# Where the time-step products, the modulation loads and the first merge stand in a two-layer attention and SSD kernel

## The chip, the cores and the metric

The kernel runs on one core of a Trainium2 chip. The metric is the device time of one execution in microseconds (us); less is better. The engines are PE (TensorE, matrix products), DVE (VectorE), ACT (ScalarE), POOL (GpSimd) and SP (SyncE, which here only starts DMA transfers). Each engine works through its own instructions strictly in their order, and waits on semaphores for the others.

## The reference, cut to what matters

```
h, hc = x, ctx                      # 1024 latent and 256 context rows of 1024
for i in (0, 1):
    shift, scale, gate = split(silu(c) @ w_ada[i] + b_ada[i])      # and the same of c_ctx
    u, uc = rms(h) * (1 + scale) + shift, rms(hc) * (1 + scale_c) + shift_c
    layer 0: q, k, v, g = split(u @ w_in); y = (windowed_attention(q, k, v) * silu(g)) @ w_out
    layer 1: z, xbc, dt = split(u @ w_in)
             xs, B, C = split(silu(conv5(xbc)))                    # 8 groups of heads
             dt = softplus(dt + bias); a = cumsum over a chunk of dt * A
             scans forward and backward over chunks of 128, started from the context's states
             y = (rms_per_group((y_f + y_b + D * xs) * silu(z)) * norm_w) @ w_out
    h = h + gate * y
out = rms(h) * final_norm_w
```

All of it is fp32. The kernel gets fp32 accuracy from three products per matrix product: each operand is split in a high and a low part (`wh`, `wl`, `uH`, `uL`).

## The kernel before, in words

Rows are kept transposed in three tiles, i = 0 and 1 (512 latent columns each) and i = 2 (256 context columns). Everything is issued from Python in one order, and a scheduler then gives each engine's queue its order; that order is fixed when the program is built. Three places matter here.

**The end of layer 0's projections and the start of attention.** `qkvg` (L571 on) loops over x = 0 to 7 for q and again for the gate g. Each `g_step` computes 24 matrix products of one tile (L246 to L248), a tanh and a product on ACT and DVE (L561, L562), and a store of the result from SP (L563, `sg<-qf`). Between the steps, `fill` issues pieces of layer 1's modulation `silu(c) @ w_ada` (`ada1`): loads of `w_ada` from SP (L192) and eight PE matmuls per piece (L195); eight small ones transpose the result (L202). The list `n = [3, 3, 3, 2]` says how many pieces follow each step. After the last step, `attention` loads the rope tables (`cos`, `sin`, L530 and L531) and the weights of its first side projections (`wr<-wg`, L239), which ACT casts (L229) and POOL subtracts (L231). POOL then clears `qz` (L721) and issues the loads of `qs` and `qz` (L635, L640) from its own queue. The first score products (L655) need these.

**The passage from layer 0 to layer 1.** The last output projection leaves 512 rows whose norm has to be taken: sums over partitions by four one-column matmuls (L363; each plain fp32 matmul leaves two records in the trace), a scale on ACT (L371), a power on POOL (L372), a diagonal `dg` on DVE (L374), its spread by an fp32 matmul (L376), a copy (L378), and eight steps of modulation (L307 to L309). Beside them the raw time steps are made: 24 products each for i = 2 and i = 0 with the weight `wdt` in a `pj` bank, and four ACT copies with bias each (L919, `dt_raw`). Then the first group's projection runs: context (L1081) and latent rows (L1091), with the time steps of i = 1 between (L1101). `dt_chain` (L921 on) computes softplus, its logarithm and the two scans on 640 columns, step by step beside the convolution taps of B (`bT`, L1003, L1007, tanh L1014, product L1015). It stores the running sums (`acs`, eight stores, L937) and the chunk totals (`eald`, twelve stores, L947 and L948) to DRAM and reads them back spread over partitions (`M`, `bw`, L1217; `eal`, L949). `merge` (L1226) joins the two masks of the first chunk on DVE, after `offset` on POOL (L1222).

**The groups.** For g = 0 to 7, PE projects B, two tiles of x, C and z (L1125) of the next group while it does the scans of this one. A transpose (L1054) of a convolved tile is evicted by ACT (L1057) into `xn` or `bn`.

Of the kernel before, what the change touches and what calls it, by code (L numbers as in the profile page):

```python
# [9 lines left out]
F32 = mybir.dt.float32  # L10
# [7 lines left out]
P = 128  # L18
# [42 lines left out]
POST = 0.5  # L61
LATE = 3.0
DTPACE = 1.0
SEGS = (1.5, 2.0, 2.0, 2.2, 2.2)
_STOP = None

# [45 lines left out]
class Kernel:  # L112
# [245 lines left out]
    def rstd_c(self, pool, acc, n, width, size=512, rout=None, dout=None):  # L358

        nc, t, ps = self.nc, self.t, self.psA  # L360
        pn = t(ps, [P, 512], F32, self.ptag)
        for b in range(n // P):
            nc.tensor.matmul(pn[:, b : b + 1], acc[:, b * P : (b + 1) * P], self.ones[:, 0:1], start=True, stop=True)  # L363
        return self.rstd_n(pool, pn, n, width, size, rout, dout)

    def rstd_n(self, pool, pn, n, width, size=512, rout=None, dout=None):

        nc, t, ps = self.nc, self.t, self.psA
        nb = n // P
        rc = t(pool, [P, 4], F32, "rc", 2)[:, :nb]  # L370
        nc.scalar.activation(rc, pn[:, :nb], AF.Identity, bias=self.eps, scale=1.0 / width)  # L371
        nc.gpsimd.tensor_tensor(rc, rc, self.half.broadcast_to([P, nb]), op=ALU.pow)  # L372
        dg = t(*(dout or (pool, [P, 512], F32, "sqt"))).rearrange("p (b n) -> p b n", b=4)[:, :nb]
        nc.vector.tensor_tensor(dg, self.ident.unsqueeze(1).broadcast_to([P, nb, P]), rc.unsqueeze(2).broadcast_to([P, nb, P]), op=ALU.mult)  # L374
        pr = t(ps, [P, 512], F32, self.ptag)
        nc.tensor.matmul(pr[:, :n], self.ones, dg.rearrange("p b n -> p (b n)"), start=True, stop=True)  # L376
# [194 lines left out]
    def qkvg(self, p, wk, wv, wvp):  # L571
# [37 lines left out]
        def fill(m):  # L609
            for f in ada[:m]:  # L610
                f()
            del ada[:m]

        n = [3, 3, 3, 2]
        for x in range(8):
            w = self.load_halves(a["wq"][x])
            for i in (2, 0):
                self.q_step(p, w, x, i)
                fill(n[x % 2 * 2 + (i == 0)])
        for x in range(8):  # L620
# [84 lines left out]
    def attention(self, c0, ckv):  # L705
# [24 lines left out]
        def out_steps(i):  # L730
# [119 lines left out]
        BUFS.update(wr=2, wh=2, wl=2)  # L850
# [70 lines left out]
    def dt_chain(self, keep, rows):  # L921
# [3 lines left out]
        nb = n // P  # L925
        dt = self.dts
        w1, w2, w3, ea = [t(p, [P, KT // 2, 256], F32, y).rearrange("p a b -> p (a b)")[:, :n] for y in ("xn4", "sz", "sz", "xn4")]
        tot = t(self.pc, [P, 8], F32, "tot", 2)[:, :nb]
        et = t(self.pc, [P, 8], F32, "tot", 2)[:, :nb]
        blocks = lambda x: x.rearrange("p (c n) -> p c n", n=P)  # L930
        v, act = nc.vector, nc.scalar.activation

        def decay():
            for o in (0, 384):
                for y in range(4):
                    d, s = y // 2, (o // 384) * 512 + 256 * (y % 2)
                    nc.sync.dma_start(self.acs_d[32 * d : 32 * d + 32, s : s + 256], w3[32 * y : 32 * y + 32, o : o + 256])  # L937

        def total():
            v.tensor_copy(tot[:64], blocks(w3)[:64, :, P - 1])  # L940
            v.tensor_copy(tot[64:], blocks(w3)[64:, :, 0])
            act(et, tot, AF.Exp)
            for y in range(4):
                d, h = y // 2, y % 2
                row = self.eal_d[0][32 * d : 32 * d + 32]
                for o, c in ((0, 2 * h), (3, 4 + 2 * h)):
                    nc.sync.dma_start(row[:, c : c + 2], et[32 * y : 32 * y + 32, o : o + 2])  # L947
                nc.sync.dma_start(row[:, 8 + h : 9 + h], et[32 * y : 32 * y + 32, 2:3])  # L948
# [5 lines left out]
        def turn(b):  # L954
# [14 lines left out]

        steps = [  # L970
            lambda: v.scalar_tensor_tensor(w1, in0=dt, scalar=-1.0, in1=dt, op0=ALU.mult, op1=ALU.min),
            lambda: act(w1, w1, AF.Exp),
            lambda: v.tensor_scalar_add(w2, w1, 1.0),
            lambda: v.tensor_scalar_add(w3, w2, -1.0),
            lambda: (act(ea, w2, AF.Ln), v.tensor_sub(w1, w1, w3)),
            lambda: v.reciprocal(w3, w2),
            lambda: v.tensor_mul(w1, w1, w3),
            lambda: v.tensor_add(w1, w1, ea),
            lambda: v.scalar_tensor_tensor(dt, in0=dt, scalar=0.0, in1=w1, op0=ALU.max, op1=ALU.add),
            lambda: v.tensor_scalar_max(w2, dt, 1.0e-38),  # L980
            lambda: (act(w2, w2, AF.Ln), v.tensor_scalar(out=w1, in0=dt, scalar1=self.aneg, scalar2=None, op0=ALU.mult)),
            lambda: v.tensor_tensor_scan(out=w3[:64], data0=keep[:64], data1=w1[:64], initial=0.0, op0=ALU.mult, op1=ALU.add),
            lambda: v.tensor_tensor_scan(out=w3[64:, ::-1], data0=keep[64:, ::-1], data1=w1[64:, ::-1], initial=0.0, op0=ALU.mult, op1=ALU.add),
            decay,
            total,
            lambda: v.tensor_sub(blocks(w1), tot.unsqueeze(2).broadcast_to([P, nb, P]), blocks(w3)),
            lambda: act(w1, w1, AF.Exp),
            lambda: v.tensor_sub(w2, w2, w3),
            lambda: v.tensor_mul(w1, w1, dt),
            lambda: act(ea, w3, AF.Exp),  # L990
            rows,
        ]
        return steps + [lambda b=b: turn(b) for b in (2, 0, 4, 3, 1)]

# [16 lines left out]
    def silu(self, raw, acc):  # L1011

        nc = self.nc
        return [lambda: nc.scalar.activation(raw, acc, AF.Tanh),  # L1014
                lambda: nc.vector.scalar_tensor_tensor(acc, in0=raw, scalar=1.0, in1=acc, op0=ALU.add, op1=ALU.mult)]  # L1015

    def front(self, g, st, post, first=None, dt=None):

# [122 lines left out]
    def ssd(self, c0):  # L1141
# [16 lines left out]
        def hd(d, g):  # L1158
            return slice(32 * d + 4 * g, 32 * d + 4 * g + 4)
# [11 lines left out]
            return xw  # L1171

        def decay(hn, h, g, c, d):
            nc.gpsimd.tensor_tensor(hn, h, self.eal[:, hd(d, g), c].unsqueeze(2).broadcast_to([P, R, HP]), op=ALU.mult)

        def flat(x):
            return x.rearrange("p r h -> p (r h)")
# [46 lines left out]
        def merge(M, bw):  # L1224

            nc.vector.copy_predicated(M, self.before.unsqueeze(1).broadcast_to([P, R, P]), bw)  # L1226
# [438 lines left out]
```

## Time and profile before

| what | us |
|---|---|
| median of 3 runs | 1812.75 |
| the three runs | 1812.54, 1812.75, 1817.5 |
| the profiled execution: its own time | 1817.81 |
| the profiled execution: its span | 1816.1 |

PE is the engine to look at: it is busy nearly all the span, so its idle stretches and the stretches at a lower granted clock are what a change can win. In the rows of the profile, a bracket after an instruction gives the idle time just before it on its engine and what ended it. `PEclk` is the granted clock of TensorE, 1.00 being full speed.

### The profile page before, as it was taken

The numbers are of one execution on the slowest core, as the hardware profiler recorded it, in microseconds if no ns is written. First come the engines' busy times: TensorE is split into PE (matmuls) and PEld (weight loads), VectorE is DVE, ScalarE is ACT, GpSimd is POOL, SyncE is SP. The second block draws the span as 40 slices with busy tenths as digits, with TensorE's granted clock in tenths as the row PEclk, the third lists the DMA queues.
The fourth block names the chain that finished last, engine by engine and source line by source line (L and its number), as shares of the span: only waits on it lengthen the run. The fifth ranks groups of instructions, "written<-read, shape, count | busy, mean of one in ns | idle before, by whom it ended". The sixth has DMA issues, their size and how long they took to land. (4 is left out here: it accounts for less than half of the span.)

```text
span 1816.1 us, 28983 instructions
## 1 busy us (share of the span) xinstructions
PE 1745.0 (96%) x10319; PEld 1500.2 (83%) x10319; DVE 1180.8 (65%) x2116; ACT 866.3 (48%) x1904; POOL 798.6 (44%) x1068
## 2 busy tenths in 40 slices
PE   6899999999999999999999999999999999999997
PEld 2697778888888887778898898989889898988886
DVE  4634426788877885684776757577675757767643
ACT  3612227777777774462444534344443434544522
POOL 2331117555575555103454545545454554554321
PEclk9999999999999999999999999999999999999998
DMA  9658856434454446222333323323333332656542
GB/s 327 230 144 258 275 177 154 111 96 105 115 151 129 122 108 220 73 52 72 75 74 82 92 70 86 79 76 77 81 93 73 82 79 77 185 163 179 165 135 70
DMA packets 212495, 227.61 MB, mean 125 GB/s; under 512 B 16384, under 2 KB 149632, under 8 KB 212352
## 3 DMA queue, kind: packets, MB, share of 16 engines
q1 hardware_dynamic: 178288, 207.12, 38.4%
q0 software_dynamic: 34064, 18.65, 5.7%
q8 instruction: 81, 1.33, 0.3%
q14 instruction: 62, 0.51, 0.1%
HBM read 190.88 MB, written 35.13 MB: 124 GB/s over the span
## 5 line engine op out<-in xcount | busy, mean ns | idle before, releaser
L246 PE MATMUL pj<-uH,wh 128*128 128x512 f32 (+1 forms) x712 | 259.3, 366 | 10.9 <-ACT uH L466 6.3
L247 PE MATMUL pj<-uL,wh 128*128 128x512 f32 (+1 forms) x712 | 245.1, 345 | 0.5 <-POOL uL L703 0.4
L248 PE MATMUL pj<-uH,wl 128*128 128x512 f32 (+1 forms) x712 | 244.5, 344 | 0.4 <-POOL wl L231 0.4
L1091 PE MATMUL pj<-uH,wl 128*128 128x512 f32 x512 | 172.8, 406 | 0.0
L1091 PE MATMUL pj<-uH,wh 128*128 128x512 f32 x512 | 171.5, 405 | 1.2 <-ACT bn L1057 0.7
L1091 PE MATMUL pj<-uL,wh 128*128 128x512 f32 x512 | 169.2, 403 | 0.0
L246 PEld LDWEIGHTS pj<-uH,wh 128*128 128x128 f32 x712 | 137.3, 193 | 37.8 <-ACT uH L466 7.7
L1125 PE MATMUL pj<-wh,uH 128*128 128x256 f32 x512 | 150.3, 294 | 9.1 <-ACT xn L1057 9.1
L1169 POOL TENSOR_TENSOR xw<-xn,dtdec 128x256 f32<-128x256 f32 x144 | 92.6, 648 | 141.4 <-PE psD L1194 106.8
L1125 PE MATMUL pj<-wh,uL 128*128 128x256 f32 x512 | 152.7, 298 | 0.0
L248 PEld LDWEIGHTS pj<-uH,wl 128*128 128x128 f32 x712 | 136.9, 192 | 18.4 <-issue 1.7
L247 PEld LDWEIGHTS pj<-uL,wh 128*128 128x128 f32 x712 | 137.5, 193 | 16.0 <-issue 3.0
L1125 PE MATMUL pj<-wl,uH 128*128 128x256 f32 x512 | 146.7, 286 | 0.0
L685 DVE TENSOR_TENSOR pl<-pt,ph 128x512 fp32r<-128x512 f32 x168 | 114.1, 688 | 47.3 <-ACT ph L684 46.3
L231 POOL TENSOR_TENSOR wl<-wr,wh 128x512 fp32r<-128x512 f32 x76 | 100.1, 1321 | 91.5 <-ACT wh L229 90.4
L659 DVE CUSTOM_DVE_ANT_0 sm<-S,mask,nsink 128x640 f32<-128x640 f32 (+2 forms) x160 | 119.2, 772 | 19.7 <-PE S L655 12.6
L661 ACT ACTIVATE sm<-sm,nm 128x640 f32<-128x640 f32 (+2 forms) x160 | 118.7, 742 | 16.5 <-DVE nm L659 15.8
L684 ACT CAST ph<-pt 128x512 fp32r<-128x512 f32 x168 | 97.4, 585 | 56.3 <-PE pt L680 52.9
L229 ACT CAST wh<-wr 128x512 fp32r<-128x512 f32 (+1 forms) x116 | 74.6, 648 | 92.1 <-PE pj L247 71.5
L1091 PEld LDWEIGHTS pj<-uH,wl 128*128 128x128 f32 x512 | 95.4, 188 | 19.1
L1091 PEld LDWEIGHTS pj<-uL,wh 128*128 128x128 f32 x512 | 95.5, 189 | 18.6
L1125 PEld LDWEIGHTS pj<-wh,uH 128*128 128x128 f32 x512 | 98.6, 193 | 13.5 <-ACT xn L1057 12.1
(338 smaller groups left out, 4815.9 us busy)
## 6 DMA issues: line engine op xcount, KB each, us to landing
wr<-w_x SPq DMA_DIRECT2D x32, 512.0 KB, 4.5
M<-acs SPq DMA_DIRECT2D x64, 256.0 KB, 5.0
bw<-acs SPq DMA_DIRECT2D x64, 256.0 KB, 5.4
wr<-w_sk SPq DMA_DIRECT2D x24, 512.0 KB, 3.7
wr<-wg SPq DMA_DIRECT2D x40, 256.0 KB, 4.5
qs<-q POOLq DMA_DIRECT2D x40, 256.0 KB, 3.9
wada<-w_ada SPq DMA_DIRECT2D x16, 512.0 KB, 7.2
wr<-wq SPq DMA_DIRECT2D x32, 256.0 KB, 2.8
```

What stands on the lines that cost most here:

```text
L229: nc.scalar.copy(h, raw)
L231: (eng or nc.vector).tensor_tensor(l, raw, h, op=ALU.subtract)
L246: self.nc.tensor.matmul(ps, lh, rh, start=first and i == 0, stop=False)
L247: self.nc.tensor.matmul(ps, lh, rl, start=False, stop=False)
L248: self.nc.tensor.matmul(ps, ll, rh, start=False, stop=last and i == n - 1)
L659: nc.vector.tensor_tensor_reduce(out=sm[:, :W], in0=Sv, in1=self.mask[:, m0 : m0 + W], scale=-SCALE, scalar=self.nsink[:, 4 * j + r : 4 * ...
L661: nc.scalar.activation(sm[:, :W], sm[:, :W], AF.Exp, bias=nm[:, r : r + 1], scale=-1.0, accum_out=sums[:, r : r + 1])
L684: nc.scalar.copy(ph, ptf)
L685: nc.vector.tensor_sub(pl, ptf, ph)
L1091: nc.tensor.matmul(raw[:, 512 * i : 512 * i + 512], l[:, k, :], r[i][:, k, :], start=k + y == 0, stop=k == KT - 1 and y == 2)
L1125: nc.tensor.matmul(pj[:, c], l, r[:, k, :], start=c % 2 + q + k + y == 0, stop=c % 2 == 1 and q == 1 and k == 3 and y == 2)
L1169: nc.gpsimd.tensor_tensor(xw, X(st, c).rearrange("p (r h) -> p r h", r=R), self.dtdec[:, c, hd(d, g)].unsqueeze(2).broadcast_to([P, R, HP] ...
```

## The change

The change has five parts.

1. The pieces of `fill` after the g steps: one behind each step for x below 4, three from x = 4 on (`late`), in place of 3, 3, 3, 2 in turn.
2. The raw time steps' products go into the score banks `S`. Those of i = 0 come in two halves, tied behind the norm's sums (`summed`) and behind its spread (`spread`), inside the list of the norm's steps.
3. The sigmoid in `dt_chain` comes from a tanh on ACT (`wr`) and two fused DVE steps, in place of a reciprocal and two products.
4. Four stores of the running sums in place of eight and two of the chunk totals in place of twelve; the totals lie in another order (`EPOS`). The rows' loads are issued ahead of the totals.
5. The first merge on DVE comes after the product that ends the convolution of C (`silu_last`).

```diff
+EPOS = (0, 1, 5, 6, 3, 4, 8, 9, 2, 7)
...
-            nc.tensor.matmul(pn[:, b : b + 1], acc[:, b * P : (b + 1) * P], self.ones[:, 0:1], start=True, stop=True)
+            self.summed = nc.tensor.matmul(pn[:, b : b + 1], acc[:, b * P : (b + 1) * P], self.ones[:, 0:1], start=True, stop=True)
...
-        nc.tensor.matmul(pr[:, :n], self.ones, dg.rearrange("p b n -> p (b n)"), start=True, stop=True)
+        self.spread = nc.tensor.matmul(pr[:, :n], self.ones, dg.rearrange("p b n -> p (b n)"), start=True, stop=True)
...
         n = [3, 3, 3, 2]
+        late = lambda x: 3 if x >= G0 else 1
...
                 self.g_step(p, w, x, i)
-                fill(n[x % 2 * 2 + (i == 0)])
+                fill(late(x))
...
-                for f in steps:
+                for f in steps[:1] + ([self.dt_first] if i == 1 else []) + steps[1:]:
...
-            for i, lo in ((2, 256), (0, 0)):
-                n = TT[i][1] // 2
-                self.dt_raw(self.dts[:, lo : lo + n], self.proj(ps, self.wdt, i), n)
+            raw = self.proj(ps, self.wdt, 2, "S")
+
+            def dt_first():
+                self.dt_raw(self.dts[:, 256:384], raw, 128)
+                out = []
+                half = self.proj_g(out, ps, [self.wdt], self.uH, self.uL, 0, "S", parts=2)
+                with self.tc.issue_after(self.summed.ins):
+                    next(half)
+                with self.tc.issue_after(self.spread.ins):
+                    next(half, None)
+                self.dt_raw(self.dts[:, :256], out[0], 256)
...
-            for o in (0, 384):
-                for y in range(4):
-                    d, s = y // 2, (o // 384) * 512 + 256 * (y % 2)
-                    nc.sync.dma_start(self.acs_d[32 * d : 32 * d + 32, s : s + 256], w3[32 * y : 32 * y + 32, o : o + 256])
+            for d in range(2):
+                for o in range(2):
+                    dst = self.acs_d[32 * d : 32 * d + 32, 512 * o : 512 * o + 512].rearrange("r (h n) -> h r n", h=2)
+                    nc.sync.dma_start(dst, w3[64 * d : 64 * d + 64, 384 * o : 384 * o + 256])
...
+            lambda: act(wr, w1, AF.Tanh, scale=-0.5),
             lambda: act(w1, w1, AF.Exp),
...
-            lambda: v.reciprocal(w3, w2),
-            lambda: v.tensor_mul(w1, w1, w3),
-            lambda: v.tensor_add(w1, w1, ea),
+            lambda: v.scalar_tensor_tensor(w1, in0=wr, scalar=1.0, in1=w1, op0=ALU.add, op1=ALU.mult),
+            lambda: v.scalar_tensor_tensor(w1, in0=w1, scalar=0.5, in1=ea, op0=ALU.mult, op1=ALU.add),
...
             decay,
+            rows,
             total,
...
-            rows,
...
-            merge(fw[0], bw.pop(0))
+        with self.tc.issue_after(self.silu_last.ins):
+            merge(fw[0], bw.pop(0))
```

What this does to the queues is shown at three places. Line numbers of the changed kernel are one to some twelve higher.

SP's queue at the start of attention, before the change. `sg_0_55<-qf_2244` is the gate of x = 4, i = 0; `sg_2_57<-qf_2295` that of x = 5, i = 2; `sg_0_55<-qf_2343` that of x = 5, i = 0. The four `wr<-wg` are the first weights of attention.

```order
L563 DMA sg_0_55_151<-qf_2244 128x512
L563 DMA sg_2_57_153<-qf_2295 128x256
L530 DMA cos_2514<-cos 128x512
L531 DMA sin_2515<-sin 128x512
L239 DMA wr_2560<-wg 128x512
L239 DMA wr_2566<-wg 128x512
L239 DMA wr_2572<-wg 128x512
L239 DMA wr_2578<-wg 128x512
L563 DMA sg_0_55_151<-qf_2343 128x512
```

The same place of SP's queue with the change; `sg_2_60<-qf_2361` is the gate of x = 6, i = 2, `sg_0_58<-qf_2396` that of x = 6, i = 0, and `sg_2_60<-qf_2454` that of x = 7, i = 2.

```order
L193 DMA wl_2400<-w_ada 128x512
L564 DMA sg_0_55_151<-qf_2310 128x512
L564 DMA sg_2_60_156<-qf_2361 128x256
L531 DMA cos_2514<-cos 128x512
L532 DMA sin_2515<-sin 128x512
L564 DMA sg_0_58_154<-qf_2396 128x512
L240 DMA wr_2560<-wg 128x512
L240 DMA wr_2566<-wg 128x512
L564 DMA sg_2_60_156<-qf_2454 128x256
L240 DMA wr_2572<-wg 128x512
L240 DMA wr_2578<-wg 128x512
```

The first two weights now stand behind the gate store of x = 6, i = 0, three projections later than before, and the next two behind that of x = 7, i = 2. The order of POOL's queue there (three subtractions, the two clears, the loads of `qs` and `qz`) is the same in both.

PE's queue around the norm's sums, before the change: the sums go straight into the 24 products of i = 0 in bank `pj_8627` (the first and last are shown), then the spread, then the first group.

```order
L248 MATMUL pj_8598<-uH_1654_6747,wdtl_8589 128x256
L363 MATMUL pt_8656<-ones_68,sqa_8275 128x1 x4
L246 MATMUL pj_8627<-uH_2034_8170,wdth_8587 128x512
...
L248 MATMUL pj_8627<-uH_2034_8170,wdtl_8589 128x512
L376 MATMUL pt_8666<-dg_2129_8664,ones_68 128x512
L1081 MATMUL psD_8771<-uH_1654_6747,wh_8765 128x256
```

With the change, twelve of the 24 stand ahead of the spread and twelve behind it, in bank `S_8643`.

```order
L249 MATMUL S_8598<-uH_1654_6747,wdtl_8589 128x256
L364 MATMUL pt_8623<-ones_68,sqa_8275 128x1 x4
L247 MATMUL S_8643<-uH_2034_8170,wdth_8587 128x512
...
L249 MATMUL S_8643<-uH_2034_8170,wdtl_8589 128x512
L377 MATMUL pt_8633<-dg_2128_8631,ones_68 128x512
L247 MATMUL S_8643<-uH_2034_8170,wdth_8587 128x512
```

DVE's queue up to the product that ends the convolution of B (`bT`), before the change: the time-step chain has come as far as the reciprocal.

```order
L1007 SCALAR_TENSOR_TENSOR bT_8798<-pj_2170_8797,cw_8721,bT_8798 128x1023
L975 TENSOR_TENSOR xn_2176_8869<-xn_2176_8869,sz_8871 128x640
L1007 SCALAR_TENSOR_TENSOR bT_8798<-pj_2170_8797,cw_8721,bT_8798 128x1022
L976 RECIPROCAL sz_8871<-sz_8870 128x640
L1015 SCALAR_TENSOR_TENSOR bT_8798<-pj_2170_8797,bT_8798 128x1024
```

With the change, the chain has gone through both scans (L991, L992) ahead of that product, and four taps of the next context tile (`cctx`) stand there too.

```order
L988 SCALAR_TENSOR_TENSOR cacc_8597<-cacc_8597,xn_2176_8869 128x640
L1016 SCALAR_TENSOR_TENSOR bT_8798<-pj_2170_8797,cw_8721,bT_8798 128x1023
L1016 SCALAR_TENSOR_TENSOR cctx_8946<-psD_8912,cw_8721,cctx_8946 128x255
L989 TENSOR_SCALAR sz_8870<-cacc_8597 128x640
L990 TENSOR_SCALAR xn_2176_8869<-cacc_8597,al_8593 128x640
L1016 SCALAR_TENSOR_TENSOR bT_8798<-pj_2170_8797,cw_8721,bT_8798 128x1022
L1016 SCALAR_TENSOR_TENSOR cctx_8946<-psD_8912,cw_8721,cctx_8946 128x255
L991 SCALAR_TENSOR_TENSOR sz_8871<-cT_8753,xn_2176_8869 64x640
L992 SCALAR_TENSOR_TENSOR sz_8871<-cT_8753,xn_2176_8869 64x640
L1016 SCALAR_TENSOR_TENSOR cctx_8946<-psD_8912,cw_8721,cctx_8946 128x254
L1025 SCALAR_TENSOR_TENSOR bT_8798<-pj_2170_8797,bT_8798 128x1024
```

More of the change, by code (lines that the diff above doesn't have):

```diff
@@ L844, in attention @@
             self.dt_setup()
-            for i, lo in ((2, 256), (0, 0)):
-                n = TT[i][1] // 2
-                self.dt_raw(self.dts[:, lo : lo + n], self.proj(ps, self.wdt, i), n)
+            raw = self.proj(ps, self.wdt, 2, "S")
[8 more added lines that the diff above has]
+                self.dt_raw(self.dts[:, :256], out[0], 256)
+            self.dt_first = dt_first
             for _ in steps[-1]():
@@ L927, in dt_chain @@
         w1, w2, w3, ea = [t(p, [P, KT // 2, 256], F32, y).rearrange("p a b -> p (a b)")[:, :n] for y in ("xn4", "sz", "sz", "xn4")]
+        wr = t(p, [P, LAT], F32, "bT")[:, :n]
         tot = t(self.pc, [P, 8], F32, "tot", 2)[:, :nb]
@@ L942, in total @@
             act(et, tot, AF.Exp)
[L943 to L948, printed above, removed]
+            for d in range(2):
+                nc.sync.dma_start(self.eal_d[0, 32 * d : 32 * d + 32].rearrange("r (h k) -> h r k", h=2), et[64 * d : 64 * d + 64])
             nc.sync.dma_start(self.eal, self.eal_d.broadcast_to([P, 64, NCH + NCC]))
@@ L1013, in silu, with prod @@
         nc = self.nc
-        return [lambda: nc.scalar.activation(raw, acc, AF.Tanh),
-                lambda: nc.vector.scalar_tensor_tensor(acc, in0=raw, scalar=1.0, in1=acc, op0=ALU.add, op1=ALU.mult)]
+        def prod():
+            self.silu_last = nc.vector.scalar_tensor_tensor(acc, in0=raw, scalar=1.0, in1=acc, op0=ALU.add, op1=ALU.mult)
+        return [lambda: nc.scalar.activation(raw, acc, AF.Tanh), prod]
     def front(self, g, st, post, first=None, dt=None):
@@ L1173, in decay @@
         def decay(hn, h, g, c, d):
-            nc.gpsimd.tensor_tensor(hn, h, self.eal[:, hd(d, g), c].unsqueeze(2).broadcast_to([P, R, HP]), op=ALU.mult)
+            nc.gpsimd.tensor_tensor(hn, h, self.eal[:, hd(d, g), EPOS[c]].unsqueeze(2).broadcast_to([P, R, HP]), op=ALU.mult)
         def flat(x):
```

## The prediction

> **What bounds the kernel now.** The first view is the page: its span and its row of PE, and the costliest group that waits regularly.
>
> ```profile
> span 1816.1 us, 28983 instructions
> PE 1745.0 (96%) x10319; PEld 1500.2 (83%) x10319; DVE 1180.8 (65%) x2116; ACT 866.3 (48%) x1904; POOL 798.6 (44%) x1068
> ...
> L1125 PE MATMUL pj<-wh,uH 128*128 128x256 f32 x512 | 150.3, 294 | 9.1 <-ACT xn L1057 9.1
> ```
>
> PE is idle for 1816.1 - 1745.0 = 71.1 us. The change adds and removes no product on PE, so only these idle times, and stretches of lower clock inside the busy time, can move the end. The second view, the waits of PE in the whole program, sorts the idle times by what ended them. These rows touch the change:
>
> ```profile
> PE pj L1125 <- ACT xn L1057: 9.1, 7, 1.3
> ...
> PE aps L195 <- DMA wl<-w_ada: 2.8, 1, 2.8
> PE pj L1054 <- DVE cacc L1015: 2.8, 2, 2.2
> ...
> PE pj L246 <- ACT cacc L919: 1.4, 1, 1.4
> PE psD L1081 <- ACT cacc L919: 1.1, 1, 1.1
> PE pj L1054 <- ACT bn L1057: 1.1, 1, 1.1
> ```
>
> One wait of 2.8 us is for a modulation load. The passage has 2.8 + 1.4 + 1.1 + 1.1, all told some 6.4 us. The groups have seven waits of 1.3 us, one in each of groups 0 to 6.
>
> **Part 1: the modulation loads.** PE's timeline at the end of layer 0's projections, and two windows of it (in a window the second last three numbers are the granted clock, the DMA share and the GB/s):
>
> ```profile
> 229.17 1.94 PE L195 MATMUL aps<-wl,cs 128*32 128x512 f32 x8 [2.84 <-DMA wl<-w_ada]
> 241.06 0.39 PE L246 MATMUL pj<-uH,wh 128*128 128x256 f32 x1
> 244.13 1.06 PE L195 MATMUL aps<-wl,cs 128*32 128x512 f32 x8
> 250.26 0.96 PE L202 MATMUL pt<-sel,qf 128*128 128x16 f32 x8
> 262.83 0.40 PE L246 MATMUL pj<-uH,wh 128*128 128x512 f32 x1
> 268.30 0.40 PE L655 MATMUL S<-kHH,qs 128*128 128x256 f32 x2
> 231.00:234.00 3.00, 3.00 (x18) 2.96 (x15) 0.00 (x0) 0.00 (x0) 0.00 (x0) 0.50 1.05 404
> 234.00:237.00 3.00, 3.00 (x12) 2.44 (x12) 0.42 (x1) 0.38 (x1) 0.00 (x0) 0.83 0.99 372
> ```
>
> PE stands 2.84 us, and from 229.17 on it runs at half clock; the second window's 0.83 puts the end of that at 234 + 1.0 = 235.0. So 5.8 us ran at half speed, which cost 2.9. With the loads spread out, each piece's load has far more time ahead of its products, and I take both losses away: PE is through with its projections at 268.30 - 2.84 - 2.9 = 262.6.
>
> But what PE does next, the first scores (L655), needs `qs`. This is its chain before, from SP's first weight load to POOL's issue, with the ACT and DVE steps of a gate:
>
> ```profile
> 246.49 7.35 SPq L239 DMA_DIRECT2D wr<-wg  x4
> ...
> 250.24 1.18 ACT L229 CAST wh<-wr 128x512 fp32r<-128x512 f32 x2 [1.60 <-DMA wr<-wg]
> 250.94 2.55 POOL L231 TENSOR_TENSOR wl<-wr,wh 128x512 fp32r<-128x512 f32 x2 [37.90 <-ACT wh L229]
> ...
> 252.16 0.59 ACT L561 ACTIVATE qf<-pj 128x512 f32<-128x512 f32 x1
> ...
> 253.96 0.68 DVE L562 SCALAR_TENSOR_TENSOR qf<-qf,pj 128x512 f32<-128x512 f32 x1
> ...
> 257.76 0.84 POOL L635 DMA_DIRECT2D qs<-q  x1
> ...
> DMA to landing us min/median/max: 3.5/5.5/5.8
> ```
>
> From the first weight's issue to the issue of `qs` pass 257.76 - 246.49 = 11.3 us: two loads, casts, POOL's subtractions, a third weight that waits for the first one's buffer, the two clears. Landing takes 5.5 to 5.8, so `qs` was there at about 263.4, 4.9 us before PE came. That slack is what the change spends. SP's queue (shown with the change) now has the first weight behind the gate store of x = 6, i = 0. Backwards from PE's end at 262.6: the last projection of 512 columns takes 268.30 - 262.83 = 5.5, that of 256 columns 244.13 - 241.06, about 3.0; the last piece's eight matmuls 1.0 and the transposes 0.8. So x = 6, i = 0 ends on PE at 262.6 - 10.3 = 252.3. Its tanh (0.59), product (0.68), the handoffs and the store's issue put the first weight at about 254.2 by my estimate, 7.7 later than before. The other link, the third weight behind the gate store of x = 7, i = 2, fits inside that: that projection ends at 256.3, its store goes out near 257.5, and the buffer comes free only near 260. So `qs` is issued near 265.5 and lands near 271.2. **PE stands about 8.6 us, and the scores start at 271.2, which is 2.9 later than 268.30.** An idle of 2.84 brought 2.9 us of half-clock loss; an idle three times as long brings at least that. Part 1 costs 2.9 + 2.9 = **+5.8 us**. Bounds: with the shortest landing seen (3.5) and no loss of clock, 0.7; with handoffs 1.3 longer, +7.1; and if the chain weren't behind the store at all, `qs` at 263.4 would leave 263.4 - 268.30 = -4.9 (the fast rival).
>
> **Part 2: the time-step products at the norm.** PE, ACT, POOL and DVE at the start of the passage:
>
> ```profile
> 741.40 0.95 PE L363 MATMUL pt<-ones,sqa 128*128 128x1 f32 x8
> ...
> 742.19 1.47 ACT L919 ACTIVATE cacc<-pj,db 32x128 f32<-32x128 f32 x4
> ...
> 744.03 1.02 POOL L372 TENSOR_TENSOR rc<-rc,half 128x4 f32<-128x4 f32 x1 [7.62 <-ACT rc L371]
> ...
> 746.05 0.69 DVE L374 TENSOR_TENSOR dg<-ident,rc 128x512 f32<-128x512 f32 x1
> ...
> 750.91 1.02 PE L376 MATMUL pt<-dg,ones 128*128 128x512 f32 x2
> 745.00:747.00 2.00, 2.00 (x6) 1.52 (x6) 1.74 (x2) 0.00 (x0) 0.04 (x1) 0.50 0.60 234
> ```
>
> In a score bank the products needn't wait for L919 to empty the `pj` bank, so the 1.4 and the 1.1 us go. Twelve products of 0.23 then run from 742.4 to 745.1, and the spread needs `dg`. The copies L919, ACT's scale, the power and the diagonal give `dg` at about 747.0: a new wait of 1.9 us, inside a stretch that loses its clock before as well (0.50). Net -0.6, PE's next row at about 752.4 rather than 753.06; -2.3 if the clock holds (then 750.8).
>
> **Part 3: the shorter softplus.** DVE in the time-step chain:
>
> ```profile
> 773.20 0.82 DVE L971 SCALAR_TENSOR_TENSOR xn<-cacc 128x640 f32<-128x640 f32 x1 [0.58 <-ACT cacc L919]
> ...
> 781.82 4.14 DVE L976 RECIPROCAL sz<-sz 128x640 f32<-128x640 f32 x1
> 785.88 1.16 DVE L1015 SCALAR_TENSOR_TENSOR bT<-pj,bT 128x1024 f32<-128x1024 f32 x1
> 786.96 0.47 DVE L1007 SCALAR_TENSOR_TENSOR cctx<-psD,cw,cctx 128x254 f32<-128x254 f32 x1
> 787.35 0.81 DVE L977 TENSOR_TENSOR xn<-xn,sz 128x640 f32<-128x640 f32 x1
> ...
> 797.81 1.47 DVE L982 TENSOR_TENSOR_SCAN sz<-cT,xn 64x640 f32<-64x640 f32 x1
> ```
>
> The reciprocal's 4.14 us leave DVE, and a tanh comes to ACT, which is busy for 48% of the span. But PE doesn't wait for the chain here: it waits for the product that ends `bT`, which is done at 785.88 + 1.16 = 787.0, and 13.8 us after the chain's first step. In the new order that stretch holds no reciprocal, but three products (0.81 each), four context taps (0.47), two narrow steps (about as long as these taps) and both scans (1.47, the second taken as the first): -4.14 + 2.4 + 1.9 + 0.9 + 3.0 = +4.1, hence 17.9. The chain starts some 2 to 3 us earlier (its input is the third set of products, which the earlier front and their place right behind `pj` move up), so `bT` is ready at about 788.5, 1.4 later than before. PE is there about 2 us earlier and stands some 4. Bounds of the delay: -1 (the taps fall into ACT's waits) and +2.
>
> **Parts 4 and 5: stores and the first merge.** SP, POOL and DVE before:
>
> ```profile
> 799.31 4.14 SPq L937 DMA_DIRECT2D acs<-sz  x8
> ...
> 819.02 1.04 POOL L1222 TENSOR_TENSOR bw<-bw,vd 128x512 f32<-128x512 f32 x1 [73.97 <-DMA bw<-acs]
> ...
> 820.09 0.73 DVE L1226 COPY_PREDICATED M<-before,bw 128x512 f32<-128x512 int32 x1 [5.11 <-POOL bw L1222]
> ...
> 822.00:825.00 3.00, 2.17 (x6) 1.21 (x6) 1.76 (x3) 3.00 (x6) 1.69 (x3) 0.52 0.46 148
> ```
>
> The merge held DVE for 5.11 us; the product of a convolved tile stood behind it, and PE's transposes waited 2.2 us for that (the row `DVE cacc L1015`), after which the clock was halved (0.52) for what I read as some 6 us, a loss of 3. The later merge takes the 2.2 and the 3 away. The stores only feed this wait, so they add nothing more. What is late next is ACT's eviction of the earlier tile, behind a cast of 1 us and a first tap: I estimate a wait of 2 us there.
>
> The passage sums to: delay at `bT` +1.4, a half clock behind that wait of 4 us +2.5, merge -5.2, eviction +2, and half of the front's -0.6 kept, -0.3. That is **+0.4**, with the bounds -6 (`bT` in time, no new loss of clock) and +3.
>
> The Trainium skill's page "TensorE: Matmul & The Clock Gate", section "HAM oscillation", says to avoid PE idle gaps above about 3.4 us, the length of the window after which the clock drops. The trace is stricter: it halved after 2.84 us and after the 2.2 of the merge, and not after the 1.3s of the groups. By the page's length the 8.6 us of part 1 cost clock and a wait somewhat shorter than my 4 at `bT` doesn't; that is the last rival.
>
> **The groups.** Nothing in the diff is aimed at them, but the scheduler's order inside a group is another: the context products of the next B come first. By its rows one eviction comes earlier than the products that wait for it, so I take the 1.3 as 1.0: 7 x -0.3 = **-2**. Bounds: all 9.1 us gone, or a second such wait in half the groups, +4.6.
>
> **The sum**: +5.8 + 0.4 - 2 = +4.2 on the profiled execution, 1817.81 + 4.2 = 1822.0. That execution is 5.1 us above the median of the three runs, so against the median the sum gives 1812.75 + 4.2 = **1817.0 us**. About 0.3% (5.4 us) is what a measurement of this kernel can tell from no change.
>
> **The rivals.**
>
> *The attention start doesn't bind.* SP's place says the weight follows the store, but if the chain behind it is shorter than I add up (POOL idle for 37.90 us before it speaks for spare time), PE goes on at 263.4 and part 1 is -4.9. With the passage at its better bound's half (-3) and the groups at -2: -9.9, 1803. Against it: the 11.3 us of chain are in the trace, and nothing in it changes.
>
> *A second wait in the groups (the slow side).* In the new order ACT takes a first tap of 1024 columns ahead of the second eviction of C's or x's tile. If PE arrives at the next products before that eviction, it waits once more per group for about as long as now, 1.3 us, 7 x 1.3 = 9.1, from the point where the eviction ends over 0 us after PE's arrival. With the 1.3s as they are: +5.8 + 0.4 + 9.1 = 15.3, 1828; with a wait of half that size, 1823.5. For it: ACT is what these waits are for already. Against it: ACT is idle half of the time.
>
> *The merge isn't what PE waits for.* If the wait for `cacc` stays (the transposes wait for the stores' effect in another way), 5.2 us don't come: 1822.
>
> *The clock holds behind the wait at `bT`.* If that wait is nearer 3 us and the clock stays (it stayed after 1.3), the 2.5 us of half clock don't come: 1814.5.
>
> **How the numbers follow.** Forecast 0.38 (1817.0, of which 0.20 within 0.3% of the median, 0.18 above it); attention start not binding 0.25 (faster); second wait in the groups 0.21 (slower); merge unchanged 0.08 (slower); clock held 0.08 (same). So faster 0.25, same 0.28, slower 0.47. The range goes from 1803, the fast rival, to 1825, a little above the slow one's smaller price; what lies beyond is about 2 in 10.
>
> **What would show each step.** Part 1: a row of L657 (the scores) with an idle of 8 to 9 us before it and `qs` or its weights as releaser, and a window at 0.50 behind it; no idle at L195. Part 2: no waits for L931's copies, one at L377 of about 2 us. Part 3: a wait of some 4 us at the first transposes (L1066). Parts 4 and 5: no idle before the merge (L1238) that PE waits for. The groups: the row of L1137 at about 7 us. It is wrong if the scores start before 266, or if PE waits in the groups for something that has no row before.

## The result, and the profile after

| kernel | median, us | runs | lowest to highest |
|---|---|---|---|
| before | 1814.79 | 4 | 1812.54 to 1817.5 |
| changed | 1834.97 | 4 | 1829.26 to 1838.53 |

The change makes the kernel slower: ratio 1.0107, with a 95% interval of 1.0085 to 1.0128. The prediction said slower as the likeliest side, but 1817.0 us and at most 1825.0. The profiled execution of the changed kernel is the fastest of its four (1829.26 us), and that of before (1817.81 us) took a little longer than any of before's four, so the two traces show 11.5 us of the 20.

The page of the changed kernel:

```profile
span 1827.6 us, 28945 instructions
PE 1748.6 (96%) x10319; PEld 1499.6 (82%) x10319; DVE 1174.1 (64%) x2115; ACT 867.1 (47%) x1903; POOL 806.3 (44%) x1068
```

PE is idle for 79.0 us (71.1 before), and the same 10319 products keep it busy 3.6 us longer. Of the waits of PE in the whole program, these are new or have changed most (the releaser, then us in all, how often, the longest):

```profile
PE S L657 <- issue: 7.5, 1, 7.5
PE psX L1264 <- POOL xw L1181: 5.7, 6, 1.0
...
PE pj L1066 <- DVE bT L1025: 3.2, 1, 3.2
PE pj L1103 <- ACT xn L1069: 3.2, 8, 1.6
PE pt L377 <- DVE dg L375: 2.6, 2, 2.1
...
PE pj L1137 <- ACT xn L1069: 2.3, 7, 0.3
```

The waits for the modulation loads at L196 and for the time-step copies are gone. In their place stand a wait before the first scores (L657), one at the spread (L377, 0.4 us before), one at `bT`'s transposes (L1066, 0.5 us before), and a new one in the groups, for POOL's `xw` (x times a decay, an operand of L1264). The groups' old wait (L1137) fell from 1.3 to 0.3 us each.

**The start of attention.** SP, POOL and PE of the changed kernel:

```profile
251.40 0.33 SPq L564 DMA_DIRECT2D sg<-qf  x1
251.82 2.12 SPq L240 DMA_DIRECT2D wr<-wg  x2
...
260.91 1.27 POOL L232 TENSOR_TENSOR wl<-wr,wh 128x512 fp32r<-128x512 f32 x1 [2.03 <-ACT wh L230]
...
263.29 0.84 POOL L637 DMA_DIRECT2D qs<-q  x1
...
267.90 0.77 PE L657 MATMUL S<-kHH,qs 128*128 128x256 f32 x2 [7.45 <-issue]
```

The first attention weight follows the gate store, `qs` is issued 263.29 - 251.82 = 11.5 us later (11.3 before), and PE stands 7.45 us. Windows of the same place:

```profile
263.00:266.00 3.00, 0.00 (x0) 0.00 (x0) 0.00 (x0) 0.00 (x0) 3.00 (x5) 0.57 0.70 208
266.00:269.00 3.00, 1.02 (x3) 0.79 (x4) 0.00 (x0) 0.00 (x0) 0.12 (x1) 0.50 1.75 225
269.00:272.00 3.00, 3.00 (x9) 2.42 (x10) 0.90 (x4) 1.09 (x4) 0.00 (x0) 0.50 0.08 5
272.00:275.00 3.00, 3.00 (x14) 2.56 (x13) 0.92 (x4) 1.53 (x5) 1.59 (x3) 0.73 0.05 9
```

By the 0.57 and the 0.73 the clock is halved from 263.4, in the middle of the idle stretch, to 273.6, nearly 6 us into the work: 10.2 us.

**The groups.** One group before, and one with the change:

```profile
1034.90:1140.70 105.80, 104.46 (x651) 93.69 (x651) 72.78 (x124) 45.09 (x106) 53.02 (x75) 1.00 0.29 81
```

```profile
1150.30:1257.40 107.10, 105.35 (x651) 93.82 (x651) 73.13 (x124) 45.43 (x106) 54.06 (x75) 1.00 0.30 79
```

The same 651 products take 1.3 us longer at full clock. PE's idle times inside this group, and the one of a group before:

```profile
1216.78 1.10 PE L1289 MATMUL psX<-xn,M 128*128 128x64 f32 x8 [0.20 <-DVE y L1268]
1239.47 0.73 PE L1103 MATMUL pj<-uH,wh 128*128 128x512 f32 x2 [0.20 <-ACT xn L1069]
1254.26 0.70 PE L1264 MATMUL psX<-xw,bn 128*128 128x256 f32 x2 [0.96 <-POOL xw L1181]
1257.35 0.39 PE L1137 MATMUL pj<-wh,uH 128*128 128x256 f32 x1 [0.34 <-ACT xn L1069]
```

```profile
1246.45 0.38 PE L1125 MATMUL pj<-wh,uH 128*128 128x256 f32 x1 [1.30 <-ACT xn L1057]
```

The idle time grows only from 1.30 to 0.20 + 0.20 + 0.96 + 0.34 = 1.70 us: the wait for `xw` is new, but the old wait lost as much. The rest of the 1.3 us is time in which the rows call PE busy; by the starts of PE's products, it lies just before these waits and once more before L1289, where a product follows the one before it later than usual. POOL and DVE where PE waits for `xw`:

```profile
1252.62 1.59 POOL L1181 TENSOR_TENSOR xw<-xn,dtdec 128x256 f32<-128x256 f32 x1
1252.32 1.42 DVE L1046 TENSOR_TENSOR wl<-wr,wh 128x1024 fp32r<-128x1024 f32 x1
```

POOL's `xw` takes 1.59 us there; the median of all 144 is some 0.61. Beside it DVE subtracts a weight's low part, with both operands in SBUF. In the trace of the changed kernel 14 of the 144 `xw` take more than 1.1 us beside such a subtraction, two in most groups, and PE waits for one of the two; in the trace of before only one does in the whole program. The order of the queues inside the groups has put the two together.

**By stage.** The marks are the starts of PE's first scores, of the norm's last sums (L363, L364) and of the z products (L1125, L1137) of groups 1 and 7, from the timelines; a column is the difference of two marks, in us. The kernels beside before and changed are those of the next section.

| kernel | to the scores | to the sums | to group 1's z | a group, mean of 6 | rest | span |
|---|---|---|---|---|---|---|
| before | 268.3 | 473.1 | 187.8 | 105.8 | 252.4 | 1816.1 |
| changed | 267.9 | 478.6 | 189.8 | 107.0 | 249.2 | 1827.6 |
| pacing alone | 275.8 | 478.2 | 187.1 | 105.8 | 252.8 | 1828.6 |
| pacing, low parts on DVE | 264.1 | 478.1 | 188.3 | 105.8 | 252.6 | 1817.7 |
| banks alone | 263.7 | 475.9 | 191.8 | 107.0 | 247.1 | 1820.5 |
| change without pacing | 264.0 | 474.8 | 190.9 | 107.0 | 247.8 | 1819.5 |
| change without banks | 273.0 | 478.6 | 189.6 | 107.1 | 249.1 | 1832.5 |
| merge alone | 266.7 | 475.0 | 182.0 | 105.8 | 250.9 | 1809.2 |

A group's period is the steadiest number: 105.8 or 107.0, nothing between. The first column isn't steady: it runs from 263.7 to 268.3 in before, the banks alone and the merge alone, whose edits all lie behind it. So part sizes are taken from the timed ratios, and the traces only for the mechanism. The first two columns together tell the pacing apart even so: 738.8 to 741.7 in the four kernels without it, 746.5 to 754.0 in the three with it, and 742.2 where the low parts are on DVE.

### The profile page after: what moved, and what is told of

Its sections match the earlier page's. It is cut to its first block, busy times and chain, and to the rows that moved or that the text cites. A ratio compares the mean times of both kernels' runs of the same rounds, so it can differ in the third digit from the quotient of the medians.

```text
span 1827.6 us, 28945 instructions
## 1 busy us (share of the span) xinstructions
PE 1748.6 (96%) x10319; PEld 1499.6 (82%) x10319; DVE 1174.1 (64%) x2115; ACT 867.1 (47%) x1903; POOL 806.3 (44%) x1068
## 5 line engine op out<-in xcount | busy, mean ns | idle before, releaser
L1181 POOL TENSOR_TENSOR xw<-xn,dtdec 128x256 f32<-128x256 f32 x144 | 106.0, 739 | 188.7 <-PE psD L1206 123.4
L1103 PE MATMUL pj<-uH,wh 128*128 128x512 f32 x512 | 166.7, 400 | 3.9 <-ACT xn L1069 3.2
L1103 PE MATMUL pj<-uH,wl 128*128 128x512 f32 x512 | 167.1, 400 | 0.0
L247 PEld LDWEIGHTS pj<-uH,wh 128*128 128x128 f32 x712 | 136.6, 192 | 37.1 <-ACT wh L230 8.0
L1137 PE MATMUL pj<-wh,uH 128*128 128x256 f32 x512 | 150.9, 295 | 2.3 <-ACT xn L1069 2.3
L1137 PE MATMUL pj<-wh,uL 128*128 128x256 f32 x512 | 148.9, 291 | 0.0
L1137 PE MATMUL pj<-wl,uH 128*128 128x256 f32 x512 | 147.1, 287 | 0.0
L1103 PEld LDWEIGHTS pj<-uH,wh 128*128 128x128 f32 x512 | 94.5, 189 | 24.0 <-ACT xn L1069 4.7
```

The lines of the kernel that those rows point to most:

```text
L247: self.nc.tensor.matmul(ps, lh, rh, start=first and i == 0, stop=False)
L1103: nc.tensor.matmul(raw[:, 512 * i : 512 * i + 512], l[:, k, :], r[i][:, k, :], start=k + y == 0, stop=k == KT - 1 and y == 2)
L1137: nc.tensor.matmul(pj[:, c], l, r[:, k, :], start=c % 2 + q + k + y == 0, stop=c % 2 == 1 and q == 1 and k == 3 and y == 2)
L1181: nc.gpsimd.tensor_tensor(xw, X(st, c).rearrange("p (r h) -> p r h", r=R), self.dtdec[:, c, hd(d, g)].unsqueeze(2).broadcast_to([P, R, HP] ...
```

## Experiments

Theory: the pacing costs by the chain from the first attention weight to `qs`; the groups cost by their queue order, whatever brings it about; the merge gains. Rivals: the scores wait for something else; the groups lose by the new layout of stores and totals, or by the banks; the softplus and the stores bring what is gained.

**Pacing alone.**

```diff
+        late = lambda x: 3 if x >= G0 else 1
-                fill(n[x % 2 * 2 + (i == 0)])
+                fill(late(x))
```

> The kernel before with the paced modulation loads alone. Theory (the chain from the first attention weight to qs binds): no idle at the modulation products, PE idle 7 to 9 us before the first scores, the clock at 0.50 for 7 to 10 us around them, the groups' period unchanged at 105.8 us; 3 to 8 us slower than before. Rival (the scores' wait comes from another part of the change): no idle there, 3 to 5 us faster.

Measured: 1828.22 us against 1815.81, ratio 1.0062 (1.0038 to 1.0086), some 11 us slower, where I had expected 3 to 8. The wait is there, and so is the clock (its waits of PE, and a window):

```profile
PE S L656 <- issue: 8.3, 1, 8.3
276.00:282.00 6.00, 5.84 (x19) 4.76 (x20) 1.82 (x8) 2.03 (x8) 0.99 (x2) 0.55 0.20 13
```

The period stays at 105.8. The theory holds, its size was too small.

**Pacing, with the low parts of the first four attention weights on DVE.** POOL's queue then has the clears and the loads of `qs` first.

```diff
-            w = self.load_halves(a[src][x], nc.gpsimd)
+            w = self.load_halves(a[src][x], nc.vector if src == "wg" and x < 2 else nc.gpsimd)
```

> The paced loads alone, and the low parts of the first four attention weights computed on DVE in place of POOL, so that POOL's queue has the two clears and the loads of qs and qz first. Theory (the first scores wait for qs, whose issue stands on POOL behind the subtractions and so behind the weights' loads): no idle above 1 us before the first scores, no half clock there; 8 to 13 us faster than the pacing alone, and -4 to +2 us against before. Rival (the wait is for something else, such as the memory of the projections' stage or the gate stores): 5 us or more of idle stay, the time within 4 us of the pacing alone.

Measured: 1816.64 us against 1816.35, ratio 1.0003 (0.9991 to 1.0015). POOL and PE of this kernel:

```profile
255.03 1.09 POOL L722 MEMSET qz<- 64x512 f32 x2 [40.61 <-issue]
256.08 0.84 POOL L636 DMA_DIRECT2D qs<-q  x1
...
264.10 0.40 PE L656 MATMUL S<-kHH,qs 128*128 128x256 f32 x2
```

`qs` is issued at 256.08, and the scores start with no idle before them. The 11 us are gone, so the chain was the whole cost of the pacing. The pacing itself then gains nothing that can be measured: before's wait for `w_ada` is 2.84 us in its one profiled execution, but 0.3 to 2.5 in the other seven kernels without pacing (the probe at the end apart), and in two of these alone the clock drops behind it.

**The same with six stores and the later merge.** The diff adds parts 4 and 5 of the change to the kernel above.

> The same with the six stores and the later first merge, without the tanh and the score banks; its groups have before's order. Theory (pacing free once qs is out of the way, merge worth about 4 us): 2 to 8 us faster than before, period 105.8. Rival (the merge's gain needs the tanh): within 2 us of the kernel with the pacing and DVE alone.

Measured: 1811.93 us against 1816.35, ratio 0.9978 (0.9966 to 0.9989). The gain comes without the tanh; whether it is the merge's or the stores' is shown further down.

**Banks alone.** Part 2 of the change, nothing else.

> The kernel before with the time-step products in the score banks alone (in two halves around the norm's spread). Theory (the queue order inside the groups, which this part alone turns into that of the changed kernel, costs the groups): period of a group 107.0 us in place of 105.8, a wait of about 1.0 us per group of the state products for POOL's xw, 7 to 10 us slower in all. Rival (the groups lose by the stores' layout or by the tanh, neither of which is in here): period 105.8, total within 3 us of before.

Measured: 1823.79 us against 1815.81, ratio 1.0033 (1.0018 to 1.0049), some 6 us slower and a little less than expected. Its waits of PE:

```profile
PE pj L1064 <- DVE bT L1025: 7.9, 1, 7.9
PE psX L1262 <- POOL xw L1179: 6.7, 7, 1.0
```

The period is 107.0 without a new layout and without a tanh, so the rival falls. The wait at `bT` is 7.9 us here, with the reciprocal still in the chain; in the whole change, with the tanh, it is 3.2. The banks have moved the time-step chain forward in DVE's queue, so that both scans stand ahead of `bT`'s product:

```profile
786.35 1.47 DVE L992 TENSOR_TENSOR_SCAN sz<-cT,xn 64x640 f32<-64x640 f32 x1
787.85 1.49 DVE L993 TENSOR_TENSOR_SCAN sz<-cT,xn 64x640 f32<-64x640 f32 x1
789.37 1.23 DVE L1025 SCALAR_TENSOR_TENSOR bT<-pj,bT 128x1024 f32<-128x1024 f32 x1
```

It is done 51.0 us after the start of the norm's sums, 45.6 before; and PE is there 2.1 us earlier.

**The change without the banks.** Parts 1, 3, 4 and 5. Its PE queue inside groups 3 to 6 is that of the changed kernel.

> The whole change without the score banks: its queues inside groups 3 to 6 are nonetheless in the changed kernel's order. Theory (the order costs, whatever part brings it about): period of a group 107.0 us, the wait for POOL's xw of 1.0 us per group is there; 14 to 20 us slower than before. Rival (the score banks themselves cost, by the memory they take or hold): period 105.8, 6 to 12 us slower.

Measured: 1834.14 us against 1816.35, ratio 1.0098 (1.0083 to 1.0113). Its waits of PE, and one group:

```profile
PE S L657 <- issue: 7.5, 1, 7.5
PE psX L1254 <- POOL xw L1171: 6.5, 7, 1.0
1155.40:1262.40 107.00, 105.28 (x650) 93.78 (x650) 73.04 (x124) 45.36 (x106) 53.95 (x75) 1.00 0.30 79
```

The period is 107.0 and the wait for `xw` is there with no bank in it. It is the order that costs, and different parts of the change lead to it. The pacing alone keeps before's order and softplus, stores and merge together keep it too; the two sets together do not. The traces leave no exception: inside groups 2 to 6 the 14 kernels have just two orders, each the same on PE, DVE, ACT and POOL. The nine with before's order have a period of 105.8 us and one or two long `xw` in the whole program; the five with the other have 107.0 us and 14 of them. The banks add nothing to this kernel that can be told from noise (1.0107 with them).

**The change without the pacing.** Parts 2 to 5.

> The whole change without the pacing. Theory (pacing costs by the chain to qs, the groups by their order, independently): no idle before the first scores, the groups' period 107.0, 5 to 12 us slower than before, and 5 to 9 us faster than the whole change. Rival (the pacing also brings the groups' order about): period 105.8, within 3 us of before.

Measured: 1821.44 us against 1815.81, ratio 1.0035 (1.002 to 1.0049). The period is 107.0 and no idle stands before the scores: pacing and order cost independently. Against the whole change that is some 13 us by the ratios, more than the 5 to 9 expected, mostly because the pacing costs more. And parts 3 to 5, which gain 4.7 us by themselves (below), gain nothing on top of the banks: 1.0035 with them, 1.0033 without.

**Softplus, stores and merge.** Parts 3, 4 and 5.

> The kernel before with the tanh in the softplus, the six stores and the later first merge, without the pacing and without the score banks; its queues inside groups 2 to 6 are in before's order on PE. Theory (order): period 105.8 us, the waits for the merge gone, 2 to 6 us faster than before. Rival (stores and totals in another layout slow POOL in the groups): period 107 us, 4 to 8 us slower.

Measured: 1810.76 us against 1815.81, ratio 0.9974 (0.9959 to 0.9988), some 4.7 us faster, period 105.8.

**Merge alone.**

```diff
-        merge(fw[0], bw.pop(0))
+        with self.tc.issue_after(self.silu_last.ins):
+            merge(fw[0], bw.pop(0))
```

> The kernel before with the later first merge alone. Theory (the merge holds DVE and so the transposes): the 2.2 us wait for cacc and often the half clock behind it go, 2 to 5 us faster than before. Rival (the shorter softplus and the stores bring the gain of parts 3 to 5): within 1 us of before.

Measured: 1808.02 us against 1816.35, ratio 0.9955 (0.9939 to 0.9972), 8 us faster and more than expected. The wait of PE for that product in this kernel, and its window at the end of the passage:

```profile
PE pj L1057 <- DVE cacc L1016: 0.6, 1, 0.6
815.00:822.00 7.00, 5.88 (x30) 4.13 (x28) 3.91 (x3) 4.27 (x7) 4.04 (x5) 1.00 0.72 136
```

The same wait was 2.8 us before, and this is before's window behind it:

```profile
822.10:828.90 6.80, 6.05 (x22) 4.55 (x23) 5.49 (x7) 3.72 (x7) 3.81 (x6) 0.50 0.64 214
```

PE was busy for 6.05 of these 6.80 us at half clock, which lost 3.0. With the 2.2 us less of waiting that is 5.2 of the 8; in this execution the clock stayed whole at the start of the passage too, where before lost 1.7.

**Merge and tanh.** Parts 3 and 5.

> The later merge and the tanh for the reciprocal, without the stores, banks and pacing; groups in before's order. Theory (the shorter softplus moves steps of the chain ahead of the taps that PE waits for, and so takes some of the merge's gain): 1 to 4 us slower than the merge alone, that is 4 to 7 us faster than before. Rival (it is the stores that take it): within 1.5 us of the merge alone.

Measured: 1811.87 us against 1814.36, ratio 0.999 (0.9976 to 1.0003); it can't be told from before, and is 3.9 us above the merge alone by the medians, and some 6 by the ratios. Waits of PE in the passage, and a window behind the second:

```profile
PE pj L1095 <- ACT bn L1061: 1.9, 1, 1.9
PE pj L1058 <- ACT bn L1061: 1.7, 1, 1.7
793.40:796.80 3.40, 3.40 (x8) 2.72 (x9) 3.34 (x4) 1.91 (x3) 0.00 (x0) 0.50 0.23 80
```

In the merge alone the same two waits are these:

```profile
PE pj L1057 <- ACT bn L1060: 1.1, 1, 1.1
...
PE pj L1094 <- ACT bn L1060: 0.7, 1, 0.7
```

With the shorter chain PE no longer waits for `bT`, but ACT, which evicts the transposes, now has a step of the time-step chain (L982) and the load of its function table ahead of the second one:

```profile
790.79 1.28 ACT L982 ACT_TABLE_LOAD   x1
792.09 0.74 ACT L982 ACTIVATE sz<-sz 128x640 f32<-128x640 f32 x1
792.73 0.57 ACT L1061 COPY bn<-pj 128x512 f32<-128x512 f32 x1
```

That is 1.8 us more of waiting, and a half clock of 3.4 us behind it. Both stand in each of the three traces with the tanh and without the banks, and in none of the three with the merge and without the tanh and the banks. So in the traces the tanh gives back part of what the merge gains, and not by the delay of `bT` that I had expected of it. The timed runs are less sure: softplus, stores and merge together have 0.9974, and the next run, which is the same without the tanh, 0.997.

**Merge and stores.** Parts 4 and 5.

> The later merge and the six stores with the rows' loads ahead of the totals, without tanh, banks and pacing; groups in before's order. Theory (with the merge out of the way nothing waits for the stores): within 1.5 us of the merge alone, 6.5 to 9.5 us faster than before. Rival (the earlier loads of the rows hold something up): 2 to 4 us slower than the merge alone.

Measured: 1808.25 us against 1814.36, ratio 0.997 (0.9956 to 0.9983); 0.2 us above the merge alone by the medians, and 2.7 by the ratios, whose intervals overlap. A cost or gain of the six stores can't be told from noise.

**Merge, and the products in the banks in one piece.**

```diff
-                self.dt_raw(self.dts[:, lo : lo + n], self.proj(ps, self.wdt, i), n)
+                self.dt_raw(self.dts[:, lo : lo + n], self.proj(ps, self.wdt, i, "S"), n)
```

> The later merge, and the time-step products in the score banks in before's place, not split around the norm's spread; its groups have the changed kernel's order on PE. Theory (the banks save the two waits of 1.4 and 1.1 us at the start of the passage, the order costs 1.2 us per group): period 107.0, the waits for the copies of the time steps gone, 2 us faster to 3 us slower than before, 6 to 11 us slower than the merge alone. Rival (only the split of the products brings the costly order about): period 105.8, 8 to 11 us faster than before.

Measured: 1825.28 us against 1814.36, ratio 1.0071 (1.0047 to 1.0095), worse than expected of either. Waits of PE:

```profile
PE psX L1255 <- POOL xw L1172: 6.7, 7, 1.0
PE pj L1057 <- DVE bT L1016: 6.2, 1, 6.2
...
PE pt L376 <- DVE dg L374: 3.8, 2, 3.4
```

The banks bring the costly order even unsplit. And both waits that they take away (1.4 and 1.1) come back larger, at the spread (3.4) and at `bT` (6.2).

**The collision by itself.** Ahead of the kernel before stands a stretch with 24 products of `xw`'s form on POOL, and beside them products and subtractions on DVE; the kernel's own work is unchanged.

```diff
+        for n in range(24):
+            nc.gpsimd.tensor_tensor(pa[n], x, f.unsqueeze(2).broadcast_to([P, 4, 64]), op=ALU.mult)
+        for n in range(8):
+            nc.vector.tensor_tensor(pm[n], acc, raw[:, :512], op=ALU.mult)      # acc in PSUM
+        for n in range(4):
+            nc.vector.tensor_sub(pl[n], raw, hi)                                # all in SBUF
```

> The kernel before with a stretch put ahead of it: 24 products on POOL of the form of xw (128x256, SBUF), and beside them on DVE first 8 products of a PSUM bank with SBUF (128x512), then 4 subtractions of the form of the weights' low part (128x1024, both operands and the result in SBUF). The total time isn't of interest. Theory (POOL's xw is slowed by a DVE subtraction that reads only SBUF, and not by one that reads PSUM): POOL's products take 0.61 us beside the PSUM products and with DVE idle, and 1.2 us or more on average beside the four subtractions. Rival (the long xw in the groups come from something else that happens at the same point, such as PE's or ACT's accesses): 0.61 us throughout.

Measured once (1825.79 us; the time isn't of interest), in groups of POOL beside the PSUM products, of POOL beside the subtractions, and of DVE:

```profile
L181 POOL TENSOR_TENSOR pa<-px,pf 128x256 f32<-128x256 f32 x9 | 5.2, 609 | 1.8 <-DVE pf L178 1.8
```

```profile
L181 POOL TENSOR_TENSOR pa<-px,pf 128x256 f32<-128x256 f32 x4 | 6.2, 1588 | 0.0
```

```profile
L188 DVE TENSOR_TENSOR pl<-praw,phi 128x1024 fp32r<-128x1024 f32 x4 | 6.1, 1591 | 0.0
L186 DVE TENSOR_TENSOR pm<-pacc,praw 128x512 f32<-128x512 f32 x8 | 4.9, 688 | 0.0
```

609 ns beside products that read PSUM, 1588 beside subtractions that read only SBUF; the 1.59 us of the group's `xw` is the same number. DVE's subtraction slows down as well, from 1.23, its median in the changed kernel, to 1.59 us. The page "SBUF — State Buffer" of the Trainium skill, section "Who interferes with whom", says that a DVE instruction with two SBUF inputs contends with a GpSimd instruction that reads SBUF. The trace agrees: in the probe the two kinds alternate, one of each every 1.55 us. They don't simply take turns, though: 0.61 and 1.23 one after the other would be 1.84. So the probe shows that the subtraction alone makes `xw` long. That removing this collision alone from the groups restores 105.8 wasn't tried; how much of the 1.3 us is the collision's, and how much the other waits of the new order, stays open.

## Why the prediction was wrong

Two steps failed: the saving that part 1 counted on, and the term of the groups.

**Part 1** was right in mechanism and too small. The chain from weight to `qs` came out at 11.5 us (11.3 forecast), the idle stretch at 7.45 (8.6), because `qs` was there 4.6 us after its issue and not 5.5 to 5.8. Of the half clock's 10.2 us, 273.6 - 267.9 = 5.7 fell into work, a loss of 2.9. That this is the 2.9 of the forecast is partly luck: it was taken over from a stretch of 6.8 us. Forecast +5.8, measured some +11 by the ratio of the pacing alone. The mis-sized term is the saving. It was taken from the one profiled execution, 2.84 us of wait and 2.9 of clock. In the seven other kernels without pacing, the probe apart, the wait is 0.3 to 2.5 us, with a mean of 1.5, and the clock stays whole there in five of them. With 1.5 of wait and no clock to save, the same sum gives 5.8 + 5.7 - 1.5 = +10.0. The fast rival, in which the attention start doesn't bind, fell with the 7.45 us of idle.

**Part 2.** The new wait at the spread is 2.1 us as forecast (1.9), and the two old waits went. The clock held there, and PE came to `bT`'s transposes 2.1 us earlier, as forecast (about 2).

**Part 3.** The wait at `bT`'s transposes is 3.2 us where I had some 4: the product is done 46.3 us after the start of the norm's sums and not 45.6, so 0.7 later (1.4 forecast). The clock was halved for 6.8 us behind it, from 792.5 on, so the rival in which it holds fell:

```profile
792.00:795.00 3.00, 1.50 (x6) 1.11 (x7) 2.94 (x6) 1.90 (x5) 0.00 (x0) 0.58 0.21 60
```

That lost 2.6 (2.5 forecast). But I put the delay down to the shorter softplus; the banks make it (a wait of 7.9 with them alone, 0.5 before), and the tanh shortens it. The tanh with the merge and no banks takes the wait at `bT` away and costs at ACT's evictions instead.

**Parts 4 and 5.** The merge's gain of 5.2 us was right in its two terms, and the merge alone measured 8. The eviction behind it waits 1.6 us (2 forecast). The stores were put at nothing, and nothing was measured that is clear of noise.

**The passage** as a whole: forecast +0.4, measured +2.0 to group 1's z in the two traces. Of that, +0.4 is up to group 0's z (832.3 - 746.5 against 826.8 - 741.4); the other 1.6 lies inside group 0.

**The groups** are the step that failed in mechanism: "By its rows one eviction comes earlier than the products that wait for it, so I take the 1.3 as 1.0: 7 x -0.3 = **-2**". That old wait did fall, to 0.3. But I looked only at the waits that existed, and the sign that I had named myself came: PE waits in the groups for something that has no row before. The new order costs 1.25 us a group, 7.5 over six groups, of which the rest of the program gives 3.2 back. The rival on the slow side had the right price (1.3 a group, 1828), but by coincidence: not a second wait for ACT's evictions but, for the most part of the new idle, POOL's `xw`, slowed by DVE. Part 1's five and the groups' six to ten us are most of what lay between 1817 and 1835.

## What to carry to other kernels

A wait in one profiled execution is a sample: before its saving is counted, ask whether other executions have it, above all when a half clock hangs on it. A change that takes load off one queue moves what stands behind it on another; follow the moved instruction to the first consumer that had slack, and count that slack as spent. Where a scheduler sets the order, look in a periodic part for new neighbours of DVE and POOL, not only for what becomes of the old waits; here one part of five, a few lines long, was worth keeping (the merge alone, 0.9955 of before), and no combination that was run beat it.

## What the runs showed of the hardware

The half-clock stretches of all traces but the last of each are multiples of one length: 3.4 us, 6.8 or 10.2. A wait of some 2 us brought one in some executions and none in others: 1.9 us for `w_ada` did in the banks alone, 2.1 didn't in the probe; and a wait of 1.17 us at the start of the passage, for the copies of the time steps, did in softplus, stores and merge and the same 1.17 didn't in the merge alone. So in these traces the price of a wait on PE of 1.1 to 2.9 us is its length plus 0, 1.7 or at most 3.4 us.

That goes some way to explain why the runs of one kernel differ by up to 10 us. Of the 25 runs of before that were timed beside the first experiments, the shortest (1810.54 us) has a mean granted clock of 0.991 and the longest (1821.0) one of 0.987; 0.004 of 1815 us are 7 of the 10 us between them. What made the timed runs of the whole change another 5 us slower than its profiled one stays open. The stage table points at the start of the program: the profiled execution reaches the scores at 267.9 us, that of the change without the banks, whose part 1 is the same, at 273.0.
